# Second-layer attention scores: two half-row F32 products replaced by whole-row F32R products of stacked halves

## The chip, the cores and the metric

The kernel runs on one core of one Trainium2 chip, in one launch. The metric is device time in microseconds (us). The kernel before took 1045.1 us in the median of three runs (1043.58 to 1045.55). One execution was profiled. TensorE is PE in the profile (its weight loads are PEld), VectorE is DVE, ScalarE is ACT, GpSimd is POOL, and SyncE, from whose queue the transfers are issued, is SP.

## The reference, cut to what matters

A two-layer decoder step is computed for 512 prompt tokens and for 8 sequences of 4 new tokens. The first layer is an RWKV-7 time mixer, the second is three-branch sparse attention (NSA) with 16 query heads and 4 key/value heads of 64 channels. The change touches the second layer's prompt part alone. For a block of 128 queries of one key/value head it computes, for each of the head's four query heads:

```python
l_c = jnp.einsum('tkgd,nkd->tkgn', qg, k_cmp) * scale + b_c
p_c = masked_softmax(l_c, (d_c >= 0)[:, None, None, :], -1)
...
l_s = jnp.einsum('tkgd,tkjsd->tkgjs', qg, kg) * scale + b_s
p_s = masked_softmax(l_s, (d_s >= 0)[:, :, None], (-2, -1))
...
l_w = jnp.einsum('tkgd,lkd->tkgl', qg, k_win) * scale + b_w
p_w = masked_softmax(l_w, valid_w[:, None, None, :], -1)
```

These are the scores against 31 compressed keys, against the selected keys and against the window's keys. With 512 prompt tokens there are 8 blocks of 64 keys and 16 may be selected, so every block is, and the window of 512 covers everything: both branches see all keys up to the query's own position. The sums over d run over 64 channels.

## The kernel before, in words

Activations are stored with channels on the 128 partitions and tokens along the free dimension (`NT` = 544 columns: 512 prompt tokens and 32 new ones). Two heads of 64 channels share one tile of 128 partitions: `PARS` names the lower half (partitions 0 to 63, `par` 0) and the upper half (64 to 127, `par` 1).

Products that need full precision at the fast rate split each operand into a rounded F32R part and the F32R rest: ACT copies (line 286), another engine subtracts (line 287), and three products high x high, high x low, low x high are added up in PSUM (`products`, line 325). The layer's 28 input projections are done so, 48 products of 128x128 by 272 columns each, from weights that are loaded in two halves (line 296), rounded on ACT and subtracted on POOL.

The second layer is `layer1`. The projections are a generator, `dense`, over the list of jobs `PLAN["JO"]`: compressed, selected and window keys and values for a pair of heads, eight tiles of queries, eight of the gate. After each a `post` function normalises or transposes. `key_rows` makes a pair's selected or window keys in a tile `own`, with key head k0 in the lower half and k0+1 in the upper, and by two transfers (line 1613) a second tile `other` with the halves exchanged. So the keys of any head are at hand on either half: `KA[k]` and `KW[k]` hold one tile for each `par`. The selected tile has 32 columns more in front, in which `compress` puts the compressed keys. `query_rows` makes `Q[m]`, tile m of the queries, with two query heads, one on each half.

`attend(k)` works through one key/value head (a pass, k = 0 to 3): for each of four blocks of 128 queries, in the order `PLAN["BO"][k]`, it runs `scores(k, b)` interleaved with `values` of the block before. Block b sees n = 128(b+1) keys. For each m of two query tiles, `scores` computes two groups of products (line 1721): `qa` against the selected keys, with 32 compressed ones in front where b < 3, so 160, 288, 416 or 512 columns, and `qb` against the window keys, 128, 256, 384 or 512 columns. Each group is two F32 matmuls, one for each half: 64 rows of queries stationary, 64 rows of keys moving. They write two PSUM banks. For b = 3 the compressed keys are done first, in four matmuls of 32 columns (line 1710). DVE adds the bias and finds the minimum (line 1729), ACT takes the exponential (line 1736), DVE or POOL scales (line 1756). `values` transposes the weights on TensorE (line 1780), copies them out of PSUM (lines 1783 and 1785) and multiplies by the values (line 1796).

While `attend(0)` to `attend(2)` run, the remaining projections and the attention of the new tokens are filled in between (`together`, with `PLAN["N"]` steps of filler to a step of attention). `attend(3)` runs beside the part of the output projection that has its inputs (`project_out`, line 1953), after `gated` (line 1968) has loaded, gated and split six tiles of the attention's output. The last two tiles are projected at the end (line 2010).

Tiles come from pools with a fixed number of buffers (`PLAN["M1"]`): "p" holds queries, keys and values, "h" the transposed weights, "a" the exponentials, "st" small columns. A planner orders the instructions of each engine when the kernel is built: by a simulated clock, of those whose inputs are ready, the one that was written first. The order on each engine is then fixed, and an instruction that waits holds those behind it on its engine or queue.

## Time and profile before

| What | Value |
|---|---|
| median of three runs | 1045.1 us |
| the profiled execution | 1046.29 us |
| its span, first to last instruction | 1044.5 us |
| mean granted TensorE clock | 0.965 |
| TensorE busy | 971.7 us, 93% |
| VectorE, ScalarE, GpSimd busy | 61%, 52%, 45% |
| line 325, the three-way products, output in "ph" | 362.4 us in 2448 products |
| line 1721, the scores | 55.2 us in 256 records |
| second layer's attention | from 640.6 us to 1031.7 us |

Busy time of TensorE counts the stretches in which at least one matmul is in the array or on its way out of it. One matmul's length contains its way through the array, so lengths overlap; the time that a product takes from the next one is read better from runs of equal products, or from the chain of waits, which cuts time at the starts of the links. A line such as 325 or 286 is that of a helper and stands for all its callers; the tile names tell them apart.

### The profile page before, as it was taken

What the parts mean: (1) busy time and instruction counts of PE and PEld (TensorE: products, weight loads), DVE (VectorE), ACT (ScalarE), POOL (GpSimd) and SP (SyncE); (2) the same over time, 40 slices, a digit from 0 to 9 for tenths busy, and PEclk for the clock granted to TensorE, in tenths of its full rate; (3) what the DMA queues carried; (4) which work ended last, traced back from release to release, by engine and by line L of the source; (5) the groups of instructions that cost most, each with busy time, mean ns of one, the idle gap of its engine ahead of it and who ended that gap; (6) DMA issues with size and microseconds to landing.
All of it is one profiled execution on the core that took longest, in us unless ns stands there. A gap on an engine that the chain in (4) does not pass through costs nothing.

```text
span 1044.5 us, 24599 instructions
## 1 busy us (share of the span) xinstructions
PE 971.7 (93%) x9429; PEld 827.5 (79%) x9429; DVE 641.8 (61%) x1468; ACT 546.8 (52%) x1294; POOL 466.4 (45%) x575
## 2 busy tenths in 40 slices
PE   5799998989889989999898799999999998998998
PEld 4799997979777868888778798998667766795876
DVE  3798578798386533556966624655674467528455
ACT  4357686555444235435544635546674466556342
POOL 5913557755830453322222555654344354244430
PEclk8799998999899989999999999999999999998999
DMA  5685425648554454645594633232534421428443
GB/s 184 196 260 203 165 86 160 194 136 225 191 151 120 138 166 136 205 134 125 147 251 146 205 109 114 79 117 81 145 86 124 103 80 51 132 79 260 155 133 108
DMA packets 149448, 153.54 MB, mean 147 GB/s; under 512 B 52946, under 2 KB 99570, under 8 KB 149074
## 3 DMA queue, kind: packets, MB, share of 16 engines
q1 hardware_dynamic: 149330, 151.97, 48.4%
q8 instruction: 74, 1.21, 0.5%
q14 instruction: 44, 0.36, 0.1%
HBM read 111.33 MB, written 43.93 MB: 149 GB/s over the span
## 4 chain that ended last, share of the span: by engine, by line
PE 54%; DVE 8%; DMA 5%; ACT 4%; issue 2%; POOL 2%; SPq 0%; DVEq 0%; POOLq 0%; ACTq 0%
PE ph L325 24%; PE pq L1721 3%; PE pw L1796 3%; PE pq L1780 3%; PE pr L1142 2%; DMA d<-dram 2%; PE ph L2010 1%; DVE l L287 1%; DMA w<-in_nwo 1%; PE ph L360 1%; DVE tmp L1044 1%; PE s L1176 1%; PE pw L1793 1%; DMA w<-in_wo 1%; ACT l L286 1%
## 5 line engine op out<-in xcount | busy, mean ns | idle before, releaser
L325 PE MATMUL ph<-x,l 128*128 128x272 f32 x2448 | 362.4, 299 | 8.9 <-DVE l L287 2.5
L325 PEld LDWEIGHTS ph<-x,l 128*128 128x128 f32 x2448 | 324.2, 192 | 44.8 <-issue 22.6
L287 POOL TENSOR_TENSOR l<-w,l 128x512 fp32r<-128x512 f32 (+2 forms) x118 | 155.4, 1329 | 145.5 <-ACT l L286 132.2
L286 ACT ACTIVATE l<-w 128x512 fp32r<-128x512 f32 (+2 forms) x160 | 93.2, 613 | 106.1 <-PE ph L325 38.6
L325 PE MATMUL pp<-x,l 128*128 128x272 f32 x768 | 112.0, 300 | 5.7 <-POOL l L287 5.7
L325 PEld LDWEIGHTS pp<-x,l 128*128 128x128 f32 x768 | 104.4, 196 | 8.3 <-POOL l L287 5.9
L1736 ACT ACTIVATE a<-a,st 128x512 f32<-128x512 f32 (+3 forms) x128 | 70.5, 553 | 30.2 <-DVE st L1729 30.0
L1729 DVE CUSTOM_DVE_ANT_0 a<-pq,tb 128x512 f32<-128x512 f32 (+3 forms) x128 | 56.8, 484 | 19.6 <-PE pq L1721 19.4
L1783 ACT ACTIVATE h<-pq 128x512 f32<-128x512 f32 x60 | 35.5, 592 | 50.2 <-PE pq L1780 50.1
L1486 DVE TENSOR_TENSOR d<-ph,RS 128x272 f32<-128x272 f32 x56 | 24.3, 438 | 60.9 <-PE ph L325 56.7
L1721 PE MATMUL pq<-p,p 64*128 64x512 f32 (+6 forms) x256 | 55.2, 497 | 1.3 <-DVE st L1729 1.3
L325 PE MATMUL pp<-t,l 128*128 128x272 f32 x384 | 54.9, 295 | 0.0
L1780 PE MATMUL pq<-cst,a 128*128 128x128 f32 x320 | 50.8, 279 | 3.7 <-ACT h L1783 1.8
L1756 DVE TENSOR_SCALAR a<-a,st 128x128 f32<-128x128 f32 (+3 forms) x112 | 53.1, 535 | 0.7
L325 PEld LDWEIGHTS pp<-t,l 128*128 128x128 f32 x384 | 50.9, 190 | 0.9
L1780 PEld LDWEIGHTS pq<-cst,a 128*128 128x128 f32 x320 | 35.9, 140 | 18.4 <-issue 11.2
L287 POOL TENSOR_TENSOR d<-d,d 128x544 fp32r<-128x544 f32 (+2 forms) x21 | 28.6, 1363 | 45.6 <-ACT d L286 32.6
L1796 PE MATMUL pw<-h,p 128*64 128x256 f32 x320 | 47.1, 392 | 1.1 <-ACT h L1783 0.6
L287 DVE TENSOR_TENSOR l<-w,l 128x512 fp32r<-128x512 f32 x42 | 37.2, 898 | 16.1 <-ACT l L286 16.0
L656 POOL TENSOR_TENSOR d<-d,d 128x544 f32<-128x544 f32 x8 | 11.1, 1383 | 58.6 <-ACT d L374 58.6
L1749 POOL TENSOR_TENSOR cc<-cc,st 128x64 f32<-128x64 f32 x32 | 11.6, 363 | 56.1 <-DVE st L1746 35.9
L794 POOL TENSOR_TENSOR RS<-RS,d 128x272 f32<-128x272 f32 x14 | 12.9, 923 | 44.1 <-ACT d L793 40.5
(414 smaller groups left out, 1980.9 us busy)
## 6 DMA issues: line engine op xcount, KB each, us to landing
w<-in_rkvz SPq DMA_DIRECT2D x64, 256.0 KB, 2.9
d<-dram SPq DMA_DIRECT2D x54, 272.0 KB, 4.5
w<-in_win SPq DMA_DIRECT2D x56, 256.0 KB, 2.9
dram<-d SPq DMA_DIRECT2D x48, 272.0 KB, 2.5
ab<-dram SPq DMA_DIRECT2D x32, 256.0 KB, 3.7
p<-in_xT SPq DMA_DIRECT2D x16, 272.0 KB, 4.3
tb<-dram SPq DMA_DIRECT2D x16, 264.0 KB, 5.3
dram<-uar SPq DMA_DIRECT2D x8, 512.0 KB, 3.6
```

Source lines behind the costliest of these rows:

```text
L286: nc.scalar.activation(hi, raw, AF.Copy)
L287: (eng or nc.gpsimd).tensor_tensor(lo, raw, hi.bitcast(F32), OP.subtract)
L325: nc.tensor.matmul((pt[h][:m, :HN] if split else pt[:m, h, :HN]), a[:, k, :m], b[:, h * HN:(h + 1) * HN], start=(k == 0 and n == 0), stop= ...
L1142: nc.tensor.matmul(pg[par][r, i], BK[r, i, par], AR[r, i].rearrange("p a b -> p (a b)"), start=True, stop=True)
L1486: self.nc.vector.tensor_tensor(o, p, r, OP.mult)
L1721: nc.tensor.matmul(p[:, par, 0:hi - lo], Q[2 * k + m][r, tk], kk[par][r, lo:hi], start=True, stop=True)
L1729: nc.vector.tensor_tensor_reduce(out=P[par][j], in0=p[:, par, :n], in1=TB[k][:, g, o:o + n], scale=-1.0, scalar=3.0e38, op0=OP.add, op1=OP ...
L1736: nc.scalar.activation(P[par][j], P[par][j], AF.Exp, scale=-1.0, bias=st[:, 0, g, j + 1:j + 2], accum_out=st[:, 1, g, j + 1:j + 2])
L1756: (nc.gpsimd if e == "p" else nc.vector).tensor_scalar(pj, pj, rr, None, op0=OP.mult)
L1780: nc.tensor.transpose(pt[:, g % 2, g // 2], PB[g][j][:, c * 128:c * 128 + 128], ident)
L1783: nc.scalar.activation(w, pt, AF.Copy)
L1796: nc.tensor.matmul(po[r], v, W[x][:, par], start=False, stop=(x == ns - 1), skip_group_check=True)
```

## The change

Each score is still the F32 product of a query head and a key head. Both are now split into a rounded F32R half and the rest, and the two parts are stacked on the 128 partitions. The keys of one head become one tile, [rounded; rest] for even heads and [rest; rounded] for odd ones. The queries of one block become two tiles: one stacked likewise, the rounded part staying on the half where the query head was, and one with its halves exchanged. With the keys one of the two gives rounded x rounded + rest x rest, the other rounded x rest + rest x rounded; both are added in PSUM, so all four terms are there.

- `stack_halves` writes the rounded half with ACT and the rest with DVE, onto the other 64 partitions. `key_rows` calls it for each key head of a pair, in place of the two exchanging transfers. `own` is a short-lived tile now.
- `stacked_queries(k, b)` stacks the four query heads of a block, two to a call of `stack_halves`, and exchanges the halves by two transfers of 64 partitions by 512 elements. `attend` calls it for the next block after the first step of `scores`, and for the first block of a pass right before its scores.
- `pair` issues, for each of two heads, two F32R matmuls with 128 rows, 128 stationary columns and the same number of moving columns as before, in place of one F32 matmul with 64 rows.
- Query tiles come in pairs, from a new pool "q" with 2 buffers, and the stacked queries from a new pool "z" with 4. "p" goes from 13 buffers to 9, "h" from 12 to 11, "st" from 4 to 3. The tiles of "a" are 512 columns wide instead of 544.

```diff
-    'M1': {'s': 6, 'p': 13, 'tb': 2, 'a': 12, 'h': 12, 'ct': 2, 'cc': 3},
+    'M1': {'s': 6, 'p': 9, 'tb': 2, 'a': 12, 'h': 11, 'ct': 2, 'cc': 3, 'z': 4, 'q': 2},
...
-        self.open(ctx, c=1, st=4)
+        self.open(ctx, c=1, st=3)
...
+        def stack_halves(dst, src, par):
+
+            (r, _), (u, _) = PARS[par], PARS[1 - par]
+            nc.scalar.activation(dst[r], src[r], AF.Copy)
+            nc.vector.tensor_tensor(dst[u], src[r], dst[r].bitcast(F32), OP.subtract)
+
+        def stacked_queries(k, b):
+
+            tk = slice(self.tok(b), self.tok(b) + 128)
+            one, two = QZ[k, b] = [self.t("z", (128, 2, 2, 128), F32R) for _ in range(2)]
+            for par in range(2):
+                stack_halves(one[:, par], Q[k][:, :, tk], par)
+            for u, par in PARS:
+                nc.sync.dma_start(two[u].bitcast(F32), one[PARS[1 - par][0]].bitcast(F32))
...
-            own, other = (t[:, 32:] for t in selected(k0)) if br == 0 else (self.t("p", (128, 512)) for _ in range(2))
-            rows = own.rearrange("p (h n) -> p h n", h=2)
+            own = KO[k0] if br == 0 else self.t("d", (128, 512))
+            rows = own[:, 32 - 32 * br:].rearrange("p (h n) -> p h n", h=2)
             self.head_norm(t, self.qkn[:, 1 + br:2 + br], (rows, slice(0, HP)), (new, slice(HP, HN)))
-            for r, par in PARS:
-                nc.sync.dma_start(other[r], own[PARS[1 - par][0]])
+            for k in range(2):
+                kk = (KA, KW)[br][k0 + k] = self.t("p", (128, 544 - 32 * br), F32R)
+                stack_halves(kk, own, k)
...
-            q = Q[m] = self.t("p")
+            if j == 0:
+                Q[k] = self.t("q", (128, 2, NT))
+            q = Q[k][:, j]
...
+            def pair(p, m, kk, lo, hi):
+                for par in range(2):
+                    for x in range(2):
+                        nc.tensor.matmul(p[:, par], QZ[k, b][x][:, par, m], kk[:, lo:hi], start=(x == 0), stop=(x == 1))
+
...
                 for m in range(2):
-                    for r, par in PARS:
-                        nc.tensor.matmul(pc[:, par, m], Q[2 * k + m][r, tk], KA[k][par][r, 0:32], start=True, stop=True)
+                    pair(pc[:, :, m], m, KA[k], 0, 32)
...
-                    for r, par in PARS:
-                        nc.tensor.matmul(p[:, par, 0:hi - lo], Q[2 * k + m][r, tk], kk[par][r, lo:hi], start=True, stop=True)
+                    pair(p[:, :, 0:hi - lo], m, kk, lo, hi)
...
-                T = [self.t("a") for _ in range(2 if b < 2 else 4)]
+                T = [self.t("a", (128, 512)) for _ in range(2 if b < 2 else 4)]
...
-            for b in PLAN["BO"][k]:
+            order = PLAN["BO"][k]
+            for n, b in enumerate(order):
+                if (k, b) not in QZ:
+                    stacked_queries(k, b)
                 s, v = scores(k, b), self.pending
+                next(s)
+                if b != order[-1]:
+                    stacked_queries(k, order[n + 1])
+                next(v, None)
+                yield
                 for _ in s:
                     next(v, None)
                     yield
```

More of the change, by code (lines that the diff above doesn't have):

```diff
@@ L1565, in layer1 @@
         oS = self.k("oS", (128, 8, 32))
-        Q, KA, KW, VS, VW, TB, CC = {}, {}, {}, {}, {}, {}, {}
+        Q, KA, KW, KO, VS, VW, TB, CC, QZ = {}, {}, {}, {}, {}, {}, {}, {}, {}
         dZ = self.DR((128, 8, NT))
@@ L1569, in layer1 @@
         dx2 = self.DR((128, 8, NT))
-        def selected(k0):
-            if k0 not in KA:
-                own, other = self.t("p"), self.t("p")
-                for t in (own, other):
-                    nc.gpsimd.memset(t[:, 31:32], 0.0)
-                for k in range(2):
-                    KA[k0 + k] = (own, other) if k == 0 else (other, own)
-            return KA[k0]
+        def stack_halves(dst, src, par):
[9 more added lines that the diff above has]
+                nc.sync.dma_start(two[u].bitcast(F32), one[PARS[1 - par][0]].bitcast(F32))
         def compress(nn, t, k0):
@@ L1595, in compress @@
             if nn == 0:
-                selected(k0)
+                own = KO[k0] = self.t("p")
+                nc.gpsimd.memset(own[:, 31:32], 0.0)
                 self.cmp_keys(self.t("h", (128, 62)), h.rearrange("p a n o -> p (a n o)"), 62, "h", PLAN["PL"],
-                              [(KA[k0 + k][par][r, 0:31], r, slice(31 * k, 31 * k + 31)) for k in range(2) for r, par in PARS])
+                              [(own[r, 0:31], r, slice(31 * k, 31 * k + 31)) for r, k in PARS])
             else:
@@ L1616, in key_rows @@
             nc.sync.dma_start(o[:, :, HP:], new)
-            for k in range(2 * br):
-                KW[k0 + k] = (own, other) if k == 0 else (other, own)
         def value_rows(br, t, k0):
@@ L1700, in scores @@
             o = 128 * (3 - b)
-            tk = slice(self.tok(b), self.tok(b) + 128)
+            def pair(p, m, kk, lo, hi):
+                for par in range(2):
+                    for x in range(2):
+                        nc.tensor.matmul(p[:, par], QZ[k, b][x][:, par, m], kk[:, lo:hi], start=(x == 0), stop=(x == 1))
             st = self.t("st", (128, 3, 4, 3))
```

## The prediction

> **What bounds the kernel now.** I read the engines' shares on the page first, then busy time by stretch, then the chain of waits through the second layer, then single groups.
>
> ```profile
> PE 971.7 (93%) x9429; PEld 827.5 (79%) x9429; DVE 641.8 (61%) x1468; ACT 546.8 (52%) x1294; POOL 466.4 (45%) x575
> ```
>
> ```profile
> core 0: us, PE busy (x) PEld busy (x) DVE busy (x) ACT busy (x) POOL busy (x), PEclk, DMA share, GB/s
> 640.00:940.00 300.00, 293.00 (x2263) 228.35 (x2262) 164.05 (x548) 174.26 (x493) 135.49 (x176) 1.00 0.34 98
> 940.00:1044.00 104.00, 94.70 (x671) 73.95 (x670) 64.36 (x216) 47.28 (x134) 33.80 (x40) 0.96 0.51 164
> ```
>
> All scores lie in these two stretches. In the first (passes k = 0 to 2) TensorE is busy 293.0 of 300 us at full granted clock, 98%, with DVE at 55%, ACT at 58%, POOL at 45%: array time freed or added there moves the end. In the second (pass 3 and the output projection) it is busy 91%, so other work is sometimes late.
>
> The chain of waits gives the array time of each group of scores, since TensorE is its link nearly everywhere (columns: start in us, length in us, what, records). An F32 product is two records of the trace (256 records of line 1721 for 128 calls), so a group of two heads is x4.
>
> ```profile
> 657.97 1.70 PE ph L325 x12
> 660.15 1.06 PE pq L1721 x4
> 661.21 1.69 PE ph L325 x12
> 662.90 0.69 PE pq L1721 x8
> ...
> 690.27 0.90 PE pq L1721 x4
> ...
> 718.02 0.85 PE pq L1721 x4
> ...
> 776.18 0.56 PE pq L1710 x8
> ...
> 803.01 0.69 PE pq L1721 x4
> ...
> 806.61 0.63 PE pq L1721 x4
> ...
> 863.87 0.87 PE pq L1780 x8
> ...
> 933.91 8.34 PE ph L325 x65
> ```
>
> The reader is to see one time per width: 512 columns 1.06 us, 416 0.90, 384 0.85, 288 0.69, 256 0.63; block 0's pair of groups (160 and 128 columns, x8) 0.69; block 3's four 32-column calls (x8) 0.56. In a long run a full-row F32R product of 272 columns takes 8.34/65 = 0.128 us. In the runs of 12 between groups of scores it takes 1.69 where 12 x 0.128 = 1.54: 0.15 us are lost per group at its edges, where the array goes from whole rows to two halves and back. Line 1780's 128x128 products, with new weights each, take 0.87/8 = 0.109.
>
> **The products: removed and added.** Each group of two F32 calls on half rows, side by side, becomes four F32R calls on whole rows, one behind the other. F32R products of other widths are in the first layer:
>
> ```profile
> 457.67 0.63 PE L709 MATMUL ph<-d,center 128*128 128x512 f32 x2
> ...
> 475.45 0.50 PE L709 MATMUL ph<-d,center 128*128 128x256 f32 x2
> ```
>
> ```profile
> L709 PE MATMUL ph<-d,center x18: 281/397/793, 382.1 to 551.6; 128*128 128x512 f32 x16, 128*128 128x256 f32 x2
> ```
>
> ```profile
> L325 PE MATMUL ph<-x,l x1397: 282/288/594, 639.8 to 1009.7; 128*128 128x272 f32 x200
> ```
>
> Median lengths are 397 ns at 512 columns (16 of 18 records) and 288 at 272: (397 - 288)/240 = 0.454 ns a column. So one product takes 0.128 + 240 x 0.000454 = 0.237 us at 512; the first row checks it (0.63 for two, less the last one's 0.397, is 0.233). Likewise 0.194 at 416, 0.179 at 384, 0.136 at 288, 0.121 at 256. Four of each against the old group: 0.95 against 1.06, 0.77 against 0.90, 0.72 against 0.85, 0.54 against 0.69, 0.48 against 0.63. Over 4 passes and 2 head pairs there are 16 groups of 512 and 8 of each other width: 16 x 0.11 + 8 x (0.13 + 0.13 + 0.15 + 0.15) = 6.2 us saved.
>
> Narrow products gain nothing. No row shows F32R under 256 columns. One bound is the 0.109 us of line 1780, which I take because the 256-column row above still runs at the F32R rate (0.50 less the last one's 0.281 is 0.22 for one product and for the start of a run). Block 0: 8 x 0.109 = 0.87 against 0.69, 8 times, 1.4 us lost. The 32-column products: 8 x 0.109 = 0.87 against 0.56, 4 times, 1.2 lost. Together 2.7. The other bound is the rate of F32, (1.06 - 0.63)/256 = 1.68 ns a column: block 0 then takes 4 x (0.27 + 0.215) = 1.94, and 10.0 + 1.2 = 11.2 us are lost. The 32-column ones stay at 0.109 in both.
>
> Edges: 48 + 8 groups at 0.15 are 8.4 us if every edge goes, and 0 if none does. Many groups stand beside line 1796, whose stationary operand has 64 columns and which stays as it is, so I take half, 4.2.
>
> TensorE: 6.2 - 2.7 + 4.2 = 7.7 us saved.
>
> **Stacking halves: added to ACT and DVE.**
>
> ```profile
> L286 ACT ACTIVATE l<-w 128x512 fp32r<-128x512 f32 x68 | 40.2, 624 | 33.6 <-PE ph L325 19.2 <-DMA w<-in_wo 6.2 <-DMA w<-in_win 5.9
> ...
> L287 DVE TENSOR_TENSOR x<-d,x 128x544 fp32r<-128x544 f32 x6 | 4.2, 712 | 0.0
> ...
> L286 ACT ACTIVATE x<-h 128x128 fp32r<-128x128 f32 x8 | 2.1, 302 | 0.7 <-DVE h L1977 0.7
> ...
> L287 DVE TENSOR_TENSOR x<-h,x 128x128 fp32r<-128x128 f32 x8 | 2.1, 286 | 0.2 <-ACT x L286 0.2
> ```
>
> Each query block takes two rounds and two rests of 64x256. Between the rows for 128 and 512 or 544 columns these are 0.41 us on ACT and 0.42 on DVE; 32 of each, 13.1 and 13.4 us. Keys: 8 rounds at 0.63 and 8 rests at 0.70, 5.0 and 5.6. ACT gets 18.1 us, DVE 19.0, and nothing is taken from either. Over the 404 us of the two stretches that raises DVE from 57% to 61% and ACT from 55% to 59%. Its cover is TensorE's dense products; with no cover it would all be late, 19 us.
>
> Two places lie open. The block after the first of pass 3 is stacked while DVE is the chain:
>
> ```profile
> 920.00:940.00 20.00, 20.00 (x168) 19.03 (x167) 3.35 (x7) 10.86 (x20) 10.51 (x9) 1.00 0.31 93
> 940.00:960.00 20.00, 17.37 (x90) 11.21 (x89) 16.90 (x50) 14.56 (x35) 8.02 (x9) 0.83 0.90 290
> ```
>
> DVE is busy 16.9 of 20 us there and the granted clock falls to 0.83 as TensorE waits. Two rounds and two rests, 1.7 us, go on the path. The first block of that pass can be stacked before 940, where DVE is busy 3.35 of 20.
>
> The other place is the first block of each pass, which no earlier block covers: its stacking is issued just before its scores. ACT, DVE and DVE again are 1.25 us, then the two exchanges:
>
> ```profile
> cl<-in_ccv SPq DMA_DIRECT2D x16, 128.0 KB, 3.5
> ...
> dram<-h SPq DMA_DIRECT2D x12, 128.0 KB, 1.9
> ```
>
> At the 1.9 to 3.5 us of 128 KB, scores are late by 3.2 to 4.8 us, 4.0 in the middle, and behind a waiting product stands everything on TensorE. The order is laid out ahead, though, and projections (line 325) can be put in front. Bounds are 0 and 4.0 for each of the four; I take 0.5, so 2.0 us.
>
> **Transfers and buffers.** 32 exchanges of 128 KB come, 8 of keys go.
>
> ```profile
> L1613 SPq DMA_DIRECT2D p<-p x8: 467/502/782, 630.5 to 748.4; - x8
> ```
>
> ```profile
> SPq L296 <- POOL l L287: 106.9, 40, 13.6
> ```
>
> 24 more issues at 0.50 are 12 us of SP's queue. An exchange waits there for DVE's rest, and the next weight load (line 296) stands behind it, then ACT's rounding, POOL's rest and the projection. SP waits 106.9 us for POOL to free weight buffers, so a late load mostly gives up waiting it would do anyway: 0, and if that cover is gone, up to the 1.25 us of stacking, 16 times, 20 us. The keys' splitting replaces an exchange by ACT and DVE work of about 1.3 us a key, less than the transfer that goes: 0. Pools "p" 13 to 9 with the queries moved to "q", "h" 12 to 11, "st" 4 to 3: no row names a wait for one of these buffers; 0, with one group of scores (1.06 us) either way.
>
> **The sum.** -7.7 + 1.7 + 2.0 = -4.0 us. The profiled execution took 1046.29 us (span 1044.5 and 1.8 around it), 1.2 above the median of 1045.1. So 1042.3 for it, and 1041 as a median.
>
> **Rivals.** A measurement of this kernel can tell about 0.2%, 2 us, from no change.
>
> Narrow F32R products run at the F32 rate. TensorE then loses 0.8 us (6.2 - 11.2 + 4.2), and 3.7 are given back: 1049.6. For it: the kernel uses F32R in no product under 256 columns that the trace shows, so nothing rules it out. Against: the 256-column row. Chance 0.21.
>
> The other side by the first blocks: each pass begins with TensorE waiting 4.0 us for an exchange. -7.7 + 1.7 + 16.0 = +10.0, 1055. It decides from 6.0/4 = 1.5 us a pass. For it: what the chain shows at 951.77, where one transfer is all that moves for 3.88 us.
>
> ```profile
> 951.77 3.88 DMA d<-dram
> ```
>
> Against: in passes 0 to 2 projections stand ready to be put in front, which is how TensorE is 98% busy there. Chance 0.12.
>
> All edges go and nothing is given back: -(6.2 - 2.7 + 8.4) = -11.9, 1033. For it: DVE's and ACT's 40% of free time. Against: line 1796's neighbours. Chance 0.13.
>
> The freed time becomes waiting: the chain of softmax, transposes and values, with 37 us more of ACT and DVE in it, takes the bound, 1045. Against: the 98%. Chance 0.09.
>
> POOL is held by DVE. Its splits of weights feed the projections:
>
> ```profile
> L287 POOL TENSOR_TENSOR l<-w,l x64: 998/1281/1455, 641.3 to 1012.8; 128x512 fp32r<-128x512 f32 x48, 128x384 fp32r<-128x384 f32 x16
> ```
>
> ```profile
> POOL l L287 <- ACT l L286: 88.7, 31, 8.0
> ```
>
> If the 19.0 us of new rests held POOL for its 42% of busy time (169.29 of 404), 8.0 us would be late: -4.0 + 8.0, 1049. Against: the longest split is 1.455 us where the median is 1.281, so no split in this trace was held for a DVE operation of 0.7, and POOL waits 88.7 us for ACT as it is. Chance 0.05. [...]
>
> **How the numbers follow.** The forecast has 0.40, with its own range of 1036 to 1045. Faster by over 0.2%: 0.37 of that and all of the 0.13: 0.50. Within: 0.03 of the forecast, 0.09, and 0.05 of the first and last rivals: 0.17. Slower: the rest, 0.33. Cases of both signs hold the chance, so the range goes from 1032, past the case with all edges, to 1053, past the two near 1049 and the lower part of the one at 1055.
>
> **What would show it.** Groups of line 1721's successor with 512 columns near 0.95 us and runs of line 325 between them near 0.128 a product show the array's part; block 0's x8 near 0.87 or near 1.94 settles the narrow ones. Idle time of TensorE before the first scores of a pass, released by a transfer, would show the rival on the other side; new waits of line 296 for DVE would show SP's queue. I am wrong if those groups shrink and TensorE's busy share in the first stretch falls below 95%.

## The result, and the profile after

The changed kernel takes 1057.65 us in the median of four runs (1057.4 to 1059.97), the kernel before 1044.34 (1042.23 to 1045.55): a ratio of 1.0115 with a 95% interval of 1.0078 to 1.0153. A second session gave 1.0103 (1.0081 to 1.0124). It is slower, where 1041 us and faster were forecast, and it lies outside the range of 1032 to 1053. Its profiled execution took 1059.97 us, with a span of 1058.2; before it was 1044.5. So 13.7 us are to be found.

The first of the views is the page's line of shares, and the two stretches of the attention, one of which now reaches to the new end:

```profile
PE 969.9 (92%) x9429; PEld 851.2 (80%) x9429; DVE 658.3 (62%) x1504; ACT 565.9 (53%) x1334; POOL 468.7 (44%) x573
```

```profile
640.00:940.00 300.00, 285.95 (x2225) 240.75 (x2224) 180.67 (x583) 189.16 (x527) 136.81 (x175) 0.99 0.38 108
940.00:1058.00 118.00, 105.86 (x777) 91.46 (x775) 67.39 (x224) 55.15 (x150) 40.66 (x45) 0.97 0.50 158
```

TensorE was busy 293.0 of the first 300 us; now it is 285.95, 95.3%, just above the 95% named as the mark of a wrong prediction, with the granted clock at 0.99 in place of 1.00. Its total of busy time is almost the same as before (971.7), though the products got shorter. The chain of waits shows that they did:

```profile
677.00 0.93 PE pq L1712 x4
677.94 1.50 PE ph L325 x12
679.44 0.84 PE pq L1712 x8
...
704.38 0.76 PE pq L1712 x4
709.61 0.76 PE pq L1712 x4
...
792.94 0.80 PE pq L1712 x8
```

Line 1712 is the scores' line now, each record a whole product. These are groups of 512, block 0 (160 and 128), 416 and 384 columns, forecast at 0.95, 0.87, 0.77 and 0.72; the last row is block 3's eight of 32 columns, forecast at 0.87. The run of 12 projections between them takes 1.50 where it took 1.69 and where 1.54 was its own time. So behind whole-row products (line 325, and the transposes of line 1790) the array does what the prediction said. Behind products with a narrower stationary operand it does not. Line 1806 is the kernel before's line 1796, the products with the values, 64 columns:

```profile
722.82 3.45 PE pw L1806 x32
726.27 0.95 PE pq L1712 x4
```

This is a group of 416 columns too, and it takes 0.95 in place of 0.76, more than the 0.90 of the kernel before. On the chain, 14 of 38 groups stand behind such products (lines 1803, 1806 and 1937), and each takes 0.19 or 0.20 us more than its width does elsewhere: 0.67 at 256 columns, 0.72 at 288, 0.90 at 384, 1.12 at 512. All of these are longer than the old groups, which took the same time behind line 1796 as elsewhere.

**The boundary of the layers.** Before, the first two bias tables (line 1687) were loaded inside layer 0, and the first product that needs a late transfer, line 1539, ran at 611.73 us (SP's queue, then TensorE, of the kernel before; columns: start, length, engine, line, what):

```profile
515.29 0.92 SPq L1687 DMA_DIRECT2D tb<-dram  x2
```

```profile
611.73 0.64 PE L1539 MATMUL pw<-d,d 32*128 32x48 f32 x4 [0.43 <-ACT d L1531]
```

After, the same tables (now line 1694) come at the boundary, ahead of the layer's first weights on the same queue. ACT, which rounds these weights, waits 9.16 us for them, and line 1531 stands behind it on ACT; gsel's load stands behind the weights on SP; TensorE waits 8.24 us:

```profile
600.38 3.25 SPq L1694 DMA_DIRECT2D tb<-dram  x6
603.72 0.38 SPq L296 DMA_DIRECT2D w<-in_win  x1
604.87 1.66 SPq L1694 DMA_DIRECT2D tb<-dram  x2
608.67 8.36 SPq L296 DMA_DIRECT2D w<-in_win  x2
617.07 0.43 SPq L1534 DMA_DIRECT2D d<-in_gsel  x1
```

```profile
614.67 0.63 ACT L286 ACTIVATE l<-w 128x512 fp32r<-128x512 f32 x1 [9.16 <-DMA w<-in_win]
...
617.88 0.18 ACT L1531 ACTIVATE d<-pw 32x48 f32<-32x48 f32 x1
```

```profile
619.66 1.05 PE L1539 MATMUL pw<-d,d 32*128 32x48 f32 x4 [8.24 <-DMA d<-in_gsel]
```

The pools lie one behind the other in memory, and "tb" stands after "p" in the plan. With four key buffers of 2176 bytes fewer, "tb" lies 8.7 KB lower on each partition. By the time at which its loads start now, that is memory which layer 0 holds to its end.

**Behind the boundary.** From line 1539 to the end the kernel before needs 432.8 us and the changed one 438.5. Stretches of this part in four kernels, with TensorE's busy time in the second column (before, after, and two of the experiments, "tables early, second query first" and "all four edits, again"):

```profile
612.00:1044.00 432.00, 414.28 (x3128) 328.32 (x3127) 238.33 (x786) 232.80 (x652) 185.38 (x231) 0.99 0.38 114
```

```profile
620.00:1058.00 438.00, 411.06 (x3128) 351.08 (x3127) 254.05 (x822) 251.46 (x692) 187.30 (x229) 0.98 0.40 120
```

```profile
612.00:1044.00 432.00, 404.92 (x3131) 343.22 (x3129) 254.01 (x822) 250.36 (x692) 188.70 (x230) 1.00 0.41 122
```

```profile
611.00:1037.00 426.00, 405.19 (x3130) 345.97 (x3128) 254.32 (x822) 250.66 (x692) 189.17 (x230) 0.99 0.42 123
```

TensorE stood still 17.7 us before (432 less 414.28) and 26.9 after: 9.2 more. Its busy time fell by 3.2 alone, because it worked more at a lower clock. In windows of a quarter of a microsecond, the kernel before has 10.2 us of busy time at a clock of 0.50 (613 to 617 and 948 to 955 us), the changed one 18.1 (620 to 627, 771 to 778 and 972 to 979 us). The same products take longer there: line 1539's four take 1.05 us after, at 0.50, and 0.64 before, at 1.00. If half of that time is lost (the author's estimate, from the two clocks read), it is 5.0 us before and 8.8 after. Without these losses the products take 414.3 - 5.0 = 409.3 us before and 411.1 - 8.8 = 402.3 after: 7.0 less. By the third row, which runs at a clock of 1.00 throughout and takes 404.92, they are 4.4 less. So products and edges save 4.4 to 7.0 us (an estimate from these rows), and the lower clock takes part of it back.

Account of the 13.7 us: 8.0 at the boundary and 9.2 of new standstill, less 3.2 of busy time, is 14.0 (the windows are cut to whole microseconds).

In the changed kernel the clock falls where TensorE has waited, and stays down while it works again:

```profile
606.00:610.00 4.00, 4.00 (x34) 3.80 (x33) 0.00 (x0) 0.00 (x0) 2.73 (x7) 1.00 1.07 220
610.00:614.00 4.00, 1.42 (x12) 1.14 (x10) 0.00 (x0) 0.00 (x0) 1.15 (x5) 0.95 1.07 188
614.00:618.00 4.00, 0.00 (x0) 0.00 (x0) 0.00 (x0) 1.60 (x4) 1.56 (x2) 0.50 0.49 110
618.00:622.00 4.00, 1.58 (x6) 1.45 (x7) 1.19 (x4) 0.06 (x1) 1.15 (x2) 0.50 0.43 151
622.00:626.00 4.00, 4.00 (x20) 4.00 (x19) 0.27 (x2) 0.00 (x0) 2.34 (x4) 0.50 0.18 70
```

```profile
768.00:772.00 4.00, 1.44 (x9) 0.84 (x8) 3.45 (x17) 3.95 (x19) 1.63 (x4) 0.83 0.54 105
772.00:776.00 4.00, 3.37 (x18) 2.22 (x19) 3.86 (x12) 1.14 (x6) 2.47 (x6) 0.50 0.22 49
```

In the first stretch the clock falls at 613.6 us, 2.2 us after the last product ahead of the wait of 8.24 us; TensorE works without a break from 621.5 us on, and the clock is back at 627.3, 5.8 us later. In the kernel before it falls at 613.3 us, 0.9 us after the last product of line 1539, when the next ones have begun, and is back at 616.7, 3.5 us after their start. The second stretch (768 us) has no long wait, only 1.44 us of work in 4: no wait there is longer than 1.74 us, and the clock fell all the same. There is a third near 972 us. Nor does every such stretch bring a dip: the kernel with the tables early and the second query first (the third row above) does 1.56 us of work between 954 and 958 us, and its clock stays at 1.00.

### The profile page after: what moved, and what is told of

Its sections match the earlier page's. It is cut to its first block, busy times and chain, and to the rows that moved or that the text cites. A ratio compares the mean times of both kernels' runs of the same rounds, so it can differ in the third digit from the quotient of the medians.

```text
span 1058.2 us, 24792 instructions
## 1 busy us (share of the span) xinstructions
PE 969.9 (92%) x9429; PEld 851.2 (80%) x9429; DVE 658.3 (62%) x1504; ACT 565.9 (53%) x1334; POOL 468.7 (44%) x573
## 3 DMA queue, kind: packets, MB, share of 16 engines
q8 instruction: 74, 1.21, 0.5%
## 4 chain that ended last, share of the span: by engine, by line
PE 43%; DVE 4%; DMA 4%; issue 2%; ACT 2%; POOL 1%; SPq 0%; POOLq 0%; DVEq 0%; ACTq 0%
PE ph L325 22%; PE pw L1806 3%; PE pq L1712 3%; PE pq L1790 3%; DMA w<-in_win 1%; PE ph L2028 1%; PE pr L1142 1%; PE pw L1803 1%; PE ph L1937 1%; DVE p L722 1%; DMA d<-dram 1%; DMA w<-in_wo 1%; PE pw L1597 1%; DVE l L287 1%; PE ph L1863 1%
## 5 line engine op out<-in xcount | busy, mean ns | idle before, releaser
L325 PEld LDWEIGHTS ph<-x,l 128*128 128x128 f32 x2448 | 328.0, 194 | 33.6 <-issue 13.3
L1712 PE MATMUL pq<-p,z 128*128 128x512 f32 (+7 forms) x288 | 58.0, 330 | 2.6 <-DVE st L1739 2.6
L1712 PEld LDWEIGHTS pq<-p,z 128*128 128x128 f32 x288 | 42.3, 190 | 12.3 <-issue 6.3
L1766 DVE TENSOR_SCALAR a<-a,st 128x128 f32<-128x128 f32 (+3 forms) x112 | 50.2, 508 | 0.6
L287 POOL TENSOR_TENSOR d<-d,d 128x544 fp32r<-128x544 f32 (+2 forms) x21 | 27.4, 1306 | 51.7 <-ACT d L286 47.3
```

What stands on the lines that cost most here:

```text
L287: (eng or nc.gpsimd).tensor_tensor(lo, raw, hi.bitcast(F32), OP.subtract)
L325: nc.tensor.matmul((pt[h][:m, :HN] if split else pt[:m, h, :HN]), a[:, k, :m], b[:, h * HN:(h + 1) * HN], start=(k == 0 and n == 0), stop= ...
L1712: nc.tensor.matmul(p[:, par], QZ[k, b][x][:, par, m], kk[:, lo:hi], start=(x == 0), stop=(x == 1))
L1766: (nc.gpsimd if e == "p" else nc.vector).tensor_scalar(pj, pj, rr, None, op0=OP.mult)
```

## The experiments

All ratios are to the kernel before, run in the same session, with 95% intervals. The last four columns are of one profiled execution each: the first product of line 1539; from there to the end; how long TensorE stood still in that part; the mean granted clock of it. One execution differs from another: line 1539 starts at 616.9 to 619.7 us in the rows with the tables late and at 609.3 to 613.2 in the others, so the 8.0 us of the boundary are good to some 2.

| Kernel | Ratio | Line 1539 at | To the end | Still | Clock |
|---|---|---|---|---|---|
| before | 1 | 611.7 | 432.8 | 17.7 | 0.99 |
| after | 1.0115 [1.0078, 1.0153] | 619.7 | 438.5 | 26.9 | 0.98 |
| after, again | 1.0103 [1.0081, 1.0124] | 619.5 | 437.2 | 27.1 | 0.98 |
| before, tables late | 1.0076 [1.0052, 1.0101] | 618.7 | 436.4 | 19.4 | 0.98 |
| after, tables early (T) | 1.0091 [1.0055, 1.0126] | 612.8 | 443.9 | 27.7 | 0.97 |
| after, second query first (Q) | 1.0118 [1.0097, 1.0139] | 619.3 | 434.0 | 27.4 | 0.99 |
| after, exchanged products last (X) | 1.0147 [1.0115, 1.0179] | 616.9 | 441.1 | 26.7 | 0.97 |
| T and stacking across passes (S) | 1.0024 [1.0000, 1.0048] | 611.9 | 434.3 | 24.9 | 0.97 |
| T, Q | 1.0002 [0.9977, 1.0027] | 612.3 | 432.1 | 27.1 | 1.00 |
| T, Q, S | 1.0023 [1.0001, 1.0046] | 613.2 | 431.6 | 25.5 | 0.99 |
| T, Q, X | 1.0026 [1.0004, 1.0047] | 611.4 | 434.6 | 27.6 | 0.99 |
| T, Q, S, X | 0.9945 [0.9926, 0.9963] | 612.2 | 426.4 | 20.6 | 0.99 |
| T, Q, S, X, again | 0.9960 [0.9938, 0.9983] | 611.1 | 426.3 | 20.8 | 0.99 |
| before, second query first | 1.0025 [0.9999, 1.0051] | 609.3 | 435.9 | 22.3 | 0.98 |

**The tables' place.** Two kernels: the changed one with the tables put back to their old offset, and the kernel before with its tables moved down.

```diff
-    'M1': {'s': 6, 'p': 9, 'tb': 2, 'a': 12, 'h': 11, 'ct': 2, 'cc': 3, 'z': 4, 'q': 2},
+    'M1': {'s': 6, 'p': 9, 'q': 2, 'tb': 2, 'a': 12, 'h': 11, 'ct': 2, 'cc': 3, 'z': 4},
```

> The changed kernel with its pools in another order: the two buffers of the query tiles (2 x 4352 bytes per partition) stand ahead of the bias tables' pool, so that with 9 key buffers the tables lie at the same offset as in the kernel before (13 x 2176 bytes after the start of the key pool). Nothing else is changed. Theory A (the tables' placement): in the changed kernel the first two bias tables lie in memory that layer 0 holds to its end, so their loads stand ahead of the second layer's first weights on SP's queue and cost the 8 us by which the first matmul of line 1539 comes later (619.7 against 611.7 us). Then here the tables load near 515 to 523 us again, line 1539 starts near 612 us, and the time falls from 1057.7 to 1047 to 1050 us: the remaining 3 to 6 us above the kernel before belong to the stacking. Rival B (what is lost at the boundary is regained later as shorter waits, and the stacked products and their operands cost it all): line 1539 comes at 612 us and the time stays at 1055 to 1058 us. Rival C (placement is the whole loss and the array's saving is real): 1041 to 1044 us.

```diff
-    'M1': {'s': 6, 'p': 13, 'tb': 2, 'a': 12, 'h': 12, 'ct': 2, 'cc': 3},
+    'M1': {'s': 6, 'tb': 2, 'p': 13, 'a': 12, 'h': 12, 'ct': 2, 'cc': 3},
```

> The kernel before with one change: the pool of the bias tables comes ahead of the key pool, 13 x 2176 bytes lower, so that the first two tables lie where layer 0 works to its end, as in the changed kernel. No product is changed. Theory A (the tables' placement costs the 8 us at the boundary): the tables load near 600 us, the first matmul of line 1529 or 1534 after the boundary comes some 8 us later, and the time rises from 1044.3 to 1051 to 1055 us. Rival B (the boundary's wait is regained later): 1043 to 1046 us.

The second is plain. Not one product of it differs from the kernel before, and it loses 0.76%, 8 us; its SP queue and TensorE show the changed kernel's boundary:

```profile
599.73 3.32 SPq L1687 DMA_DIRECT2D tb<-dram  x6
603.15 0.38 SPq L296 DMA_DIRECT2D w<-in_win  x1
```

```profile
618.67 1.06 PE L1539 MATMUL pw<-d,d 32*128 32x48 f32 x4 [7.77 <-DMA d<-in_gsel]
```

So theory A stands for it: an offset in memory costs 8 us. (The edit moves the key pool up as well; the times of the loads tie the loss to the tables.) The first kernel loads its tables from 514.9 us again and brings line 1539 back to 612.8, and yet takes 1.0091. That is rival B's time, but not for rival B's reason: nothing was regained in waits. TensorE stands still as long as in the changed kernel (27.7 us against 26.9 and 27.1), but is busy for 415.3 us where the changed kernel's two profiles have 411.1 and 408.9. So in this execution the 7 us gained at the boundary went into a lower clock, 0.97. Its stretches show where; those of the next experiment are at 1.00 in the same places:

```profile
760.00:800.00 40.00, 35.29 (x270) 27.88 (x270) 26.38 (x101) 26.04 (x85) 13.83 (x25) 0.91 0.41 108
...
920.00:980.00 60.00, 55.28 (x392) 47.63 (x392) 37.02 (x117) 37.08 (x97) 27.75 (x28) 0.94 0.53 165
```

**The second query tile.** Where a stacked block needs both query tiles, the first scores wait for the second tile's norm; the edit puts that tile one job earlier, on top of the early tables, and then alone on the changed kernel.

```diff
-('q', 0), ('kw', 0), ('q', 1), ('vs', 0)
+('q', 0), ('q', 1), ('kw', 0), ('vs', 0)
```

> The kernel with the tables early again, and one step more: in the order of the second layer's first rows, the second query tile comes ahead of the window keys (kc, ks, q, q, kw in place of kc, ks, q, kw, q). A stacked block holds both query tiles of a key head, and so the first scores wait for the norm of the second query tile, two ACT and two DVE steps of stacking and the exchange transfer; the kernel before needed only the first tile. Theory A (the late second tile holds up the first scores): the first scores product comes 3 to 6 us earlier than in the kernel with the tables early alone, and the time falls by 2 to 4 us against it. Rival B (the rows that go on meanwhile fill TensorE, and the end is set by its total work): within 1.5 us of the kernel with the tables early.

> The changed kernel with only the second query tile ahead of the window keys in the order of the second layer's first rows; the bias tables stay where the changed kernel has them. Theory A (tables and query order are two separate losses that add up): the tables' 8 us remain and the later start of the scores is repaired, 8 to 10 us less than the changed kernel in the same session, less the tables' share: 1050 to 1055 us. Rival B (the order of the queries is nearly the whole loss, and the wait at the boundary is regained later): 1045 to 1049 us. Rival C (each repair is worth nothing without the other): 1055 to 1060 us.

With the tables early the first scores product starts at 646.6 us in place of 659.3, and the time falls by 0.89%, 9.3 us, far more than theory A's 2 to 4: TensorE stands still as long as in the changed kernel (27.1), but its clock no longer falls. Alone, on the changed kernel, the same order is worth nothing (1.0118 against 1.0103): rival C. Nor are the early tables alone (1.0091). So either lateness by itself keeps the kernel at 1.009 to 1.012, both together cost hardly more, and only both repairs bring it to 1.0002. With the tables late it is the boundary's 7 us and 2 behind it; with the second query late it is busy time at a lower clock, and hardly anything else. Why the two don't add up in the changed kernel is not settled.

That order by itself does not help the kernel before:

> The kernel before with only the second query tile ahead of the window keys in the order of the second layer's first rows: what that order is worth where a score needs only its own query tile. Theory A (the order matters because a stacked block needs both tiles): within 0.2% of the kernel before, 0.998 to 1.002. Rival B (the order is better for any kernel, and the repaired kernels owe their time to it and not to stacked products): 0.994 to 0.997.

1.0025 is a little above theory A's 0.998 to 1.002 and far from rival B's gain: the order pays only in the stacked kernel, whose blocks need both tiles.

The chain of the kernel with both repairs shows what a first block costs when nothing covers it, from the query's norm to its scores:

```profile
642.73 0.97 DVE q L1503
...
643.72 0.42 ACT z L1574
...
644.17 1.02 DVE z L1575
...
645.85 2.37 DMA z<-z
...
648.36 1.72 PE pq L1712 x10
```

**Stacking ahead, and the order of the four products.** With both faults repaired the kernel stands at 1.0002: TensorE is busy 9.4 us less than in the kernel before, 5.0 of them because that one's clock dipped, and it stands still 9.4 us longer. Two edits aim at that. S stacks the first block of passes 1 to 3 while the pass before ends; X puts both products with the stacked queries ahead of those with the exchanged ones, so that two of four need no transfer.

```diff
                 if b != order[-1]:
                     stacked_queries(k, order[n + 1])
+                elif k < 3:
+                    until(("q", 2 * k + 2), ("q", 2 * k + 3))
+                    stacked_queries(k + 1, PLAN["BO"][k + 1][0])
```

> The kernel with the tables early again, and one step more: the first block of passes 1, 2 and 3 is stacked during the last block of the pass before, as the other blocks are, and not just ahead of its own scores. Theory A (the first blocks' stacking stalls TensorE 2 to 4 us each, as the prediction's third rival has it): the time falls by 4 to 10 us against the kernel with the tables early alone. Theory B (as the prediction took it, 0.5 us each): 1 to 2 us less. Rival C (the queries and rows that are then due earlier hold up the last block of the pass before): 0 to 3 us more.

> Tables early, second query first, and the first block of passes 1 to 3 stacked during the last block of the pass before. The kernel with the first two alone stood at a ratio of 1.0002 to the kernel before; stacking across the passes, added to the tables alone, took 0.7% off. Theory A (the first blocks' stacking stalls TensorE at three pass starts): 2 to 5 us faster than with the first two alone, ratio 0.995 to 0.998. Rival B (that gain was of the lower clock's dips, not of the stall): ratio 0.999 to 1.002.

```diff
-                for par in range(2):
-                    for x in range(2):
+                for x in range(2):
+                    for par in range(2):
```

> As the kernel beside it (tables early, second query first, stacking across passes), with the four products of a group in another order: both products with the stacked queries first, then both with the exchanged ones, so that the first two don't wait for the exchange transfer (2.37 us at the first scores of pass 0). Theory A (the exchange is on the path of first blocks): 1 to 3 us less than the kernel beside it. Rival B (it is covered once the stacking is ahead, the only bare place being pass 0): 0 to 1 us less. Rival C (a product that leaves its bank open while another bank is written costs more switching, some 0.05 us in each of 72 groups): up to 3 us more.

> The kernel with tables early, second query first, stacking across the passes and both products with the stacked queries first, once more: its 0.9945 [0.9926, 0.9963] came from six runs of one session, and three of its four edits without the fourth stood at 1.0002 to 1.0026. Theory A (the stacked products' 7 us come to light only when no wait grows; its TensorE waits after 560 us sum to 26.8 us as in the kernel before, 27.1 us, against 33 to 36 us in its neighbours): 0.992 to 0.997 again. Rival B (a chance of one session): 0.998 to 1.003.

> The changed kernel with one edit: in a group of products both with the stacked queries come first and both with the exchanged queries last; tables and query order stay as the changed kernel has them. Theory A (the order of the four products is what the array's gain was lost to, wherever it is applied): 7 to 9 us less than the changed kernel, ratio to the kernel before 1.002 to 1.005. Rival B (it pays only where the scores' start is on time and the blocks are stacked ahead): ratio 1.008 to 1.012, as without it.

> Tables early, second query first, and both products with the stacked queries first in a group, but no stacking across the passes. With stacking across the passes this stood at 0.9945 [0.9926, 0.9963]; without the product order and without stacking across at 1.0002. Theory A (the product order is worth 0.8% by itself): 0.992 to 0.996. Rival B (product order and stacking across are worth something only together): 0.998 to 1.001.

S with early tables alone takes 0.7% off (theory A's size), but its standstill fell by only 2.8 us. It leaves the second query late (the first scores start at 655.1 us) and yet comes to 1.0024, where the second query's order came to 1.0002; and with S in, that order adds nothing (1.0023). So the late second query costs its 9 us only where the first blocks of the later passes are stacked late as well. The clock does not decide it either: over the whole of all executions its mean is 0.964 with T, 0.971 with T and Q, 0.970 in the kernel before, but 0.963 with T and S, which is 0.7% faster than T. How much of T's loss the clock's dips make is open. Added to both repairs, S and X are worth nothing one by one (1.0023 and 1.0026), and X on the changed kernel makes it, if anything, slower. Together they give 0.9945 and, in another session, 0.9960: 4 to 6 us below the kernel before. Standstill is 20.6 us there, near the 17.7 of the kernel before. This is the only version in which the products' saving reaches the end. Rival C of the run with X, costlier changes between banks (its 0.05 us a group was the author's guess, from no row), is out: groups of 512 columns behind whole-row products take 0.91 to 0.93 us there and 0.93 to 0.95 with T and Q alone. Against the kernel with T and Q, the standstill that goes lies in 700 to 860 us (these rows are of all four edits, again, and then of T and Q):

```profile
700.00:760.00 60.00, 59.76 (x477) 50.21 (x476) 38.16 (x121) 40.67 (x109) 27.52 (x34) 1.00 0.43 119
760.00:800.00 40.00, 36.98 (x283) 27.81 (x282) 27.03 (x99) 27.71 (x90) 14.59 (x25) 0.96 0.31 87
800.00:860.00 60.00, 60.00 (x481) 51.20 (x481) 35.60 (x108) 38.81 (x98) 32.79 (x37) 1.00 0.49 134
```

```profile
700.00:760.00 60.00, 58.52 (x469) 47.40 (x468) 39.43 (x138) 40.63 (x114) 23.62 (x33) 1.00 0.43 117
760.00:800.00 40.00, 34.94 (x264) 25.03 (x261) 27.04 (x95) 27.91 (x87) 18.13 (x26) 1.00 0.28 81
800.00:860.00 60.00, 57.92 (x448) 48.54 (x447) 31.63 (x93) 35.24 (x92) 29.26 (x35) 1.00 0.45 124
```

That is 5.4 of 6.3 us. Why it takes both S and X was not isolated: the planner sets a new order of the whole layer with each edit.

**What the stacking and the products are worth.** Both on the kernel with T and Q.

> The kernel with tables early and second query first, in which only the first block of each pass stacks its queries; the other three blocks of a pass use the first one's operands, so their scores are those of the wrong queries. All products, all key stacking and all else stay; 12 of the 16 query stackings go (24 of 32 ACT steps of 0.41 us, 24 of 32 DVE steps of 0.50 us, and 12 exchanges). Theory A (the operands' work on ACT and DVE and the exchange sit on the chains that end the waits near 760, 880 and 950 us): 4 to 8 us less than with all stackings, so that the array's gain of some 7 us comes to light. Rival B (the stacking ahead is covered, and the array's gain is lost to chains that were there before): within 2 us of it.

> The kernel with tables early and second query first, with one stacked product in place of two: the products with the exchanged queries are left out, so the scores lack the terms rounded x rest and rest x rounded. Half of line 1712's 288 products go. Their groups take some 50 us in all, so TensorE's work falls by some 24 us. Theory A (TensorE's work sets the end through most of the second layer, so array time saved is time saved): 17 to 24 us less than the same kernel with both products, 1023 to 1030 us. Rival B (the softmax, sample and norm chains on ACT, DVE and POOL set the end in several stretches, so that part of the saving becomes waits): 5 to 14 us less, 1033 to 1042 us, with TensorE's idle time after 640 us up by 10 us or more. By the same share the 7 us that the change takes off the array would have been worth 2 to 4 us.

Without 12 of the 16 stackings of queries: 0.9982 [0.9966, 0.9997], 2 us less than with all, which is not clear of noise: rival B. TensorE's standstill hardly moves (25.9 us of 431). So the stacking as such is mostly covered, as the prediction had it.

With half the products: 0.9888 [0.9859, 0.9917], 1.14% or 12 us less than with all. In the profiled part TensorE's busy time is 388.11 of 416 us at a clock of 0.98, against 404.92 at 1.00: by clock, 24.6 us of work went. About half of array time saved is time saved, towards the upper end of rival B's 5 to 14 us; standstill, 27.9 us, did not grow by its 10.

**Keeping TensorE busy at the boundary.** Four times dead products were put into the changed kernel, to fill the 8 us in which it waits and so to keep the clock.

```diff
+        pd = self.t("pq", (128, 2, 512))
+        for _ in range(36):
+            nc.tensor.matmul(pd[:, 0], late[:48], X[0][0][:48, 0:512], start=True, stop=True)
```

> The changed kernel with 35 dead products of 512 columns put on TensorE ahead of the first matmuls of line 1539: they fill the 8.24 us in which it waits for the transfer of gsel (35 x 0.23 us = 8 us), and nothing reads them. Theory A (a granted clock that falls after an idle stretch of some microseconds): in the windows behind the boundary (610 to 630 us) the clock stays at 0.9 to 1.0 in place of 0.64 to 0.68, and the time falls by 2 to 4 us against the changed kernel in the same session, though more work is done. Rival B (the clock's dips have nothing to do with the wait): it dips there as before, and the time is equal or up to 2 us longer. Rival C (the dead products only bring a later transfer or a bank to wait for): 2 to 6 us longer.

> The changed kernel with 30 dead products of 512 columns whose weights are made from line 1524's outputs, so that the order of TensorE puts them right behind the transposes of line 1527 and ahead of the products of line 1539 (now 1544): at 0.23 us each they fill some 7 of the 8.2 to 8.6 us in which TensorE waits there for gsel. Nothing reads them. In the changed kernel the granted clock goes to 0.50 at 614 us and back to 1.00 at 628 us. Theory A (the clock is halved after some 3 us with little work and comes back after some 7 us with work): the windows between 614 and 628 us show 1.00 nearly throughout, and the time falls by 2 to 4 us against the changed kernel (ratio to the kernel before 1.0065 to 1.009 in place of 1.0103). Rival B (the dip has another cause): it stays, and the time is the same or up to 2 us longer. [...]

> The changed kernel with 30 dead products of 512 columns behind the transposes of line 1527, whose weights DVE makes from line 1524's outputs into a buffer that is free then, so that they don't stand behind ACT's wait for the first weights; at 0.23 us each they run from about 612 to 619 us, in the wait for gsel, and nothing reads them. Theory A (the clock is halved after some 3 us with little work and comes back after some 5 to 7 us with work): the clock between 614 and 628 us stays at 1.00 and the time falls by 2 to 4 us against the changed kernel, ratio 1.007 to 1.009 in place of 1.0103. Rival B (the dip has another cause): it stays at 0.50 there, and the time is the same or up to 2 us longer.

> The changed kernel with 36 dead products of 512 columns (48 rows deep) whose weights DVE makes from the gate's values, so that the order of TensorE puts them between line 1524 and the products of line 1539, before ACT's wait for the first weights can hold them up: 8 us in which TensorE waits in the changed kernel; nothing reads them. (In the two tries before, the dead products stood behind ACT's wait, came after the idle stretch, and cost their full time.) Theory A (the clock is halved after some 3 us with little work): the clock stays at 1.00 from 608 to 630 us and the time falls by 2 to 4 us against the changed kernel, ratio 1.007 to 1.009 in place of 1.0103. Rival B (the dip has another cause): it stays at 0.50 in 614 to 628 us, and the ratio at 1.010 to 1.013.

The first three say nothing on the clock. The planner put the first 35 at 574 to 585 us, and in the next two the dead products' weights came behind ACT's wait for the layer's first weights, so they ran from 617.6 us on, after the wait. They measure something else: 8.7 us of dead work ahead of the boundary, and 9.3 and 9.1 us behind the wait, made the ratio 1.0206, 1.0231 and 1.0238, or 11 to 14 us above the changed kernel. Array time added near the boundary was paid in full and more.

The fourth did fill the wait: TensorE is busy without a break, from 602.7 us on with products of 48 rows. The clock fell all the same:

```profile
602.00:606.00 4.00, 4.00 (x19) 3.18 (x18) 0.00 (x0) 0.00 (x0) 2.21 (x6) 1.00 1.07 226
606.00:610.00 4.00, 4.00 (x13) 2.98 (x12) 0.00 (x0) 0.63 (x1) 1.27 (x1) 0.57 0.78 156
610.00:614.00 4.00, 4.00 (x12) 2.85 (x11) 0.00 (x0) 1.04 (x3) 1.27 (x1) 0.50 0.34 110
614.00:618.00 4.00, 4.00 (x18) 3.66 (x18) 0.97 (x4) 0.00 (x0) 0.00 (x0) 0.50 0.16 55
```

Its ratio is 1.0170 [1.0138, 1.0203], beyond rival B's 1.013 as well. So theory A in the form in which it was written, that a busy TensorE keeps its clock, is refuted for products that use 48 of 128 rows. Its two lengths, some 3 us to the fall and 5 to 7 to the return, were the author's estimate, and no run shows them as fixed: the dip that was to be prevented has 2.2 and 5.8 us, the one at 613 us of the kernel before 0.9 and 3.5. No run got full-row products into the wait. That the wait causes the dip is therefore argued from its place in the traces, not shown by an experiment.

## Why the prediction was wrong, point by point

In short: the array's saving was there, at 4.4 to 7.0 us where 7.7 were forecast. Two terms at or near nothing failed, the pools (0, measured 8.0 us at the boundary) and the first blocks (2.0 us, without the second query tile), and so did the premise that freed array time moves the end (9.2 us of new standstill).

- **The products (6.2 - 2.7 us) and the edges (4.2).** Of the right size in their sum. Groups of 512, 416 and 384 columns take 0.93, 0.76 and 0.76 us in the rows shown, against 0.95, 0.77 and 0.72 (other groups of 384 take 0.70); projections between them take 1.50 where 1.54 was the value with no edge left. Half of the edges was taken because of the neighbours of line 1796, and these do keep an edge, 0.19 or 0.20 us at 14 of 38 groups. The edges' share of the saving was not measured by itself.
- **The rival of narrow F32R products at the F32 rate** is false: block 0's x8 takes 0.84 us, not 1.94. The bound that was taken, 0.109 us from line 1780, is within 4% of the 0.105 measured.
- **"Pools ...: no row names a wait for one of these buffers; 0, with one group of scores (1.06 us) either way."** This step failed. It asked whether fewer buffers would make somebody wait, and not what lies behind a pool in memory. Moving "tb" cost 8.0 us at the boundary, and 0.76% in a kernel in which no product was changed. No rival had it.
- **The first blocks (0.5 us each, bounds 0 and 4.0).** The chain of a bare one is there, with 1.02 us of DVE and 2.37 us of transfer on it. What was missed is that a stacked block needs both query tiles: the first scores of the second layer start at 665.5 us in place of 641.4, of which the boundary is 8.0. The order of two jobs, which no term had, moves them by 12.7 us with the tables early, and the time by 9.3. This is the second step that failed. Stacking across the passes (S) takes off nearly as much as that order, so it is not the one tile alone.
- **"Transfers and buffers ... 0".** The exchanges' waits are small (1.3 us in the fastest version), and SP's queue did not become the bound: line 296 waits 83.3 us for POOL in the changed kernel (640 to 1044 us), where it waited 106.9 before, and none of its waits for DVE is among the seven longest. But the order of products behind the exchange counts, with stacking across the passes: 1.0023 and 1.0026 against 0.9945.
- **The second block of pass 3 (1.7 us)** was not tested by itself.
- **The rival "the freed time becomes waiting" (0.09)** is nearest to what happened behind the boundary: 9.2 us of standstill against 4.4 to 7.0 us of products. It was argued away with the 98%, from which the prediction took that "array time freed or added there moves the end". That premise is the third thing that failed: with half the products, 24.6 us of array work bring only 12 us. The 98% held for the kernel before and its order of work; that the longer chains broke it is argued from the new waits, and no run shows it by itself. Nor was the clock in any sum: the prediction read 0.83 in one stretch and made no term of it.
- **The rival in which DVE holds POOL (0.05)** has the right pair of engines and mostly the wrong victim. POOL's splits keep their median (1.282 us, 1.281 before), and the longest grows from 1.455 to 1.780. It is DVE's subtractions that take longer beside POOL's operations:

```profile
L1575 DVE TENSOR_TENSOR z<-q,z x32: 418/421/1214, 662.9 to 998.7; 64x256 fp32r<-64x256 f32 x32
...
L1575 DVE TENSOR_TENSOR p<-p,p x4: 720/1076/1702, 643.6 to 744.3; 64x544 fp32r<-64x544 f32 x4
```

```profile
643.64 3.17 DVE L1575 TENSOR_TENSOR p<-p,p 64x544 fp32r<-64x544 f32 x2 [0.51 <-ACT p L1574]
```

```profile
643.19 3.03 POOL L287 TENSOR_TENSOR l<-w,l 128x512 fp32r<-128x512 f32 x2 [2.38 <-ACT l L286]
```

A key's subtraction takes 0.72 us at its shortest, and two beside two of POOL's take 3.17. Line 1575's queries take 16.0 us in all where 32 x 0.42 = 13.4 were forecast. Four of the 32 take more than 0.43 us: 1.12 (from 695.92 us), 1.21 (791.74) and 1.03 (997.67), which begin while a split of POOL's runs and end 0.27 or 0.28 us after it, and 0.85 (679.79) beside a scaling on POOL (line 1766). What ties the two engines together no run shows. These lengths come to some 4 us of DVE's time (an estimate: 2.6 of the queries and 1.7 of the two keys); that it lies on the path was not shown.

## What to carry to other kernels

Where a change alters the number or size of buffers, look at which tiles move in memory and whose memory they move into: a load that moves from far ahead of a boundary to the boundary costs its place in the queue (8.0 us here). When operands are merged, list what the first product now waits for that it did not before, and move that work ahead in the same edit. And a saving on the bounding engine reaches the end only if its waits do not grow; here it took four edits together to bring out 4 to 6 us.

## What the runs showed of the hardware

- In the stretches read closely (608 to 620 and 942 to 958 us before; 606 to 632, 766 to 781 and 968 to 982 us after) the TensorE clock is 1.00 or 0.50, but for the windows in which it changes. Dips lasted some 3.5 us (613 to 617 us before), 7 (948 to 955 us before) and 14 (614 to 627 us after). One followed a wait of 8.24 us, one a stretch of short waits with 1.44 us of work in 4, and one came under 48-row products with no wait at all (606 to 620 us in the fourth run with dead products); 1.56 us of work in 4 brought none (954 to 958 us with T and Q). Two kernels with the same standstill (27.7 and 27.1 us) have mean clocks of 0.97 and 1.00, and 415.3 and 404.9 us of busy time for the same products.
- F32R products of 160 and 128 columns take 0.105 us each (0.84 for eight), of 32 columns 0.10 (0.80 for eight), of 416 columns 0.19 (0.76 for four): at the narrow end the time no longer follows the columns.
- Four F32R products take 0.19 or 0.20 us more behind products whose stationary operand has 64 or 32 columns (0.95 for 416 columns, 0.76 behind whole-row products). Two F32 products on half rows take the same time behind both (0.90).
- A two-input DVE subtraction of 0.42 us takes 1.12 (at 695.92 us), and one of 0.72 up to 1.70 (at 645.11), beside a two-input POOL operation (splits of 1.31 us from 695.46 and of 1.77 from 644.45).
